# Where the weight chunks begin in SBUF: one offset for all jobs, or one for each layer and kind of job

## Chip, cores and metric

The kernel runs on one core of one Trainium2 chip. The metric is device microseconds of one execution, as the median of several runs.

## What is computed

A decoder trunk of two layers on one sequence of 256 tokens and 2048 channels, all in float32. Each layer normalises its input, projects it to 7692 columns, runs three mixers on parts of them (a convolution module, a gated delta rule, a dilated window attention), gates and concatenates their outputs and projects them back:

```
for l in range(DEPTH):
    h = rms_norm(x, norm_w[l])
    u = h @ w_in[l].astype(h.dtype)
    ...
    y = jnp.concatenate([y_conv, y_gdn, y_att], axis=-1)
    x = x + y @ w_out[l].astype(y.dtype)
return rms_norm(x, final_norm_w)
```

The convolution module has one more product, of 512 by 512 (`conf_pw_w`). The change touches the big products alone: `h @ w_in`, the 512 by 512 one, and `y @ w_out`.

## The kernel before

**Three products for one.** Every float32 operand of a big product is split into a high part (rounded to float32r) and a low part (what is left). A matmul of the reference becomes three float32r matmuls into the same PSUM tile: high by high, low by high, high by low. The activations stand in SBUF as `HT` (normalised input) and `YT` (mixer outputs), two tiles each, high and low, with the channels on the partitions: 16 blocks of 128 channels, each a slice of 256 tokens (1024 bytes).

**Weights.** They come from HBM in chunks of 128 partitions, two blocks of 128 rows each (one block each for the first two chunks of the program's first job), by SP's DMA queue into one of four `RAW` buffers. `split_weights` (lines 414 to 430) then has ACT write the high part into one of three `WHI` buffers (tile `whi`, line 191) and DVE the low part into one of three `WLO` buffers (tile `wlo`, line 199). A chunk fills its buffer from the buffer's first byte (line 422); the second block of a chunk follows the first at n x 4 bytes, n being the job's columns (384, 512, 396 or 256).

**Jobs.** `project` (line 468) walks through a list of jobs; each is one block of weight columns against all 16 (for `conf_pw_w` 4) blocks of channels. `unit` (line 442, its matmuls at line 455) is one block of 128 channels in one job. There are two kinds:

- channel-row jobs (`chan` is True): the result has channels on its rows. The weights are the stationary operand, 128 columns at a time, and 256 tokens of `HT` or `YT` move. The trace names them `acc<-HT,whi` and `acc<-HT,wlo` (moving operand first). They are the convolution's and the delta rule's inputs, the attention gate and `conf_pw_w`.
- token-row jobs (`chan` is False): the result has tokens on its rows. 128 tokens of `HT` or `YT` are stationary, and 384, 396, 512 or 256 weight columns move: `acc<-whi,HT` and the like. They are the gate `GZ` (384 and 396 columns), the attention's q, k and v, and `w_out`.

Each matmul has its own weight load (PEld), which runs while the matmul before it still streams its moving operand. The program's very last job (`"last"`) keeps its split weights in the two `HT` tiles, which are free by then; its matmuls are at line 464 and don't use `WHI` and `WLO`.

**Order.** A planner (`Plan`) writes the order of all engines from fixed costs: whichever task can start first goes next. Small matmuls and transposes of the mixers (lines 232, 239 and 754, tiles `mix`) are put between the units of the jobs.

**Addresses.** In bytes of a partition: `HT` and `YT` begin at 18432, 34816, 51200 and 67584, all multiples of 512; the four `raw` buffers at multiples of 4096 past 100352, also multiples of 512. `gap0` (64 bytes, line 263) lies before the weight buffers, so the six of them begin 64 bytes past a multiple of 512 (the first at 116800, then every 4096 bytes). `gap1` (448 bytes) brings the tiles behind them back to multiples of 512 (`b768_0` at 141824). 128 columns of float32 are 512 bytes, and so are the steps between stationary slices, tokens and channel blocks multiples of 512; in the 396-column job alone the chunk's second block begins 1584 bytes on, 48 more than a multiple of 512.

Of the kernel before, what the change touches and what calls it, by code (L numbers as in the profile page):

```python
# [11 lines left out]
F32 = mybir.dt.float32  # L12
F32R = mybir.dt.float32r
# [162 lines left out]
def hybrid_trunk(ctx, tc, x, x_t, w_in, conf_pw_w, w_out, params, final_norm_w, rope, lnc, out):  # L176
    nc = tc.nc
    cp = ctx.enter_context(tc.tile_pool(name="consts", bufs=1))
    wp = ctx.enter_context(tc.tile_pool(name="weights", bufs=1))
# [74 lines left out]
    def many(n, cols, name, dt=F32, pool=None):  # L254
        return Slots([(pool or sp).tile([128, cols], dt, name=f"{name}{i}", tag=f"{name}{i}") for i in range(n)])
# [4 lines left out]
    HT = [cp.tile([128, KB, S], F32R, name=f"HT{i}") for i in range(2)]  # L260
    YT = [cp.tile([128, KB, S], F32R, name=f"YT{i}") for i in range(2)]
    RAW = Slots([wp.tile([128, 1024], F32, name=f"raw{i}") for i in range(4)])
    wp.tile([128, 16], F32, name="gap0")
    WHI = Slots([wp.tile([128, 1024], F32R, name=f"whi{i}") for i in range(3)])
    WLO = Slots([wp.tile([128, 1024], F32R, name=f"wlo{i}") for i in range(3)])
    wp.tile([128, 112], F32, name="gap1")
    S768 = many(14, 768, "b768_")
    S1024 = many(3, 1024, "b1024_")
    S512 = many(2, 512, "b512_")
# [79 lines left out]
    chunks = []  # L349
    raw_ready, w_ready, w_gone = [], [], []  # L350

    def add_chunks(w, c0, n, order, keep):


        first = len(chunks)
        wt, rows, base = w
        base += rows * c0
        for k, m in order:
            src = bass.AP(tensor=wt.tensor, offset=wt.offset + base + (k // 2) * 256 * n + (k % 2) * n,
                          ap=[[2 * n, 128]] + ([[256 * n, m // 2]] if m > 2 else []) + [[1, min(m, 2) * n]])  # L360
            chunks.append((src, m, n, k if keep else None))
            for lst in (raw_ready, w_ready):
                lst.append([Event(), None])
        return first

    def load_xt(k0, m):

        buf = yield ("get", S768)
        yield ("dma", 128 * m * S * 4 / 330.0, lambda: nc.sync.dma_start(  # L369
            buf[:, :m * S], bass.AP(tensor=x_t.tensor, offset=x_t.offset + k0 * S, ap=[[KB * S, 128], [1, m * S]])))  # L370
        plan.spawn(norm_xt(k0, m, buf), 2)
# [9 lines left out]
    def load_x(j):  # L381

        c0, n = X_PIECES[j]
        buf = yield ("get", S768)
        xs = buf[:, :NT * n].rearrange("p (t c) -> p t c", t=NT)
        yield ("dma", 128 * NT * n * 4 / 330.0, lambda: nc.sync.dma_start(
            xs, xf[:, c0:c0 + n].rearrange("(t p) c -> p t c", p=128)))
        plan.spawn(sums_x(j, xs, buf), 3)
        if j == len(X_PIECES) - 1:
            nc.sync.dma_start(lncs, lnc)  # L390
            nc.sync.dma_start(ropes, rope.rearrange("(t p) c -> p t c", p=128))
# [4 lines left out]

    def load_weights(order):
        for i in order:
            src, m, n, _ = chunks[i]
            if i in XT_BEFORE:  # L400
                yield from load_xt(*XT_BEFORE[i])
            if i in X_BEFORE:
                yield from load_x(X_BEFORE[i])
            raw = yield ("get", RAW)
            view = raw[:, :m * n].rearrange("p (a n) -> p a n", n=n)
            flat_ = raw[:, :m * n]
            if m > 2:
                flat_ = flat_.rearrange("p (a n) -> p a n", n=2 * n)
            raw_ready[i][1] = (raw, view)
            yield ("dma", 128 * m * n * 4 / 330.0,  # L410
                   lambda src=src, flat_=flat_: nc.sync.dma_start(flat_, src))  # L411
            yield ("set", raw_ready[i][0])

    def split_weights(order):
        for i in order:
            src, m, n, keep = chunks[i]
            yield ("wait", raw_ready[i][0])
            raw, view = raw_ready[i][1]
            if keep is None:
                hb = yield ("get", WHI)  # L420
                lb = yield ("get", WLO)
                hi, lo = (b[:, :m * n].rearrange("p (a n) -> p a n", n=n) for b in (hb, lb))
                w_ready[i][1] = (hi, lo, hb, lb)
            else:
                hi, lo = (b[:, keep:keep + m, :] for b in HT)
                w_ready[i][1] = (hi, lo, None, None)
            e = Event()
            plan.spawn(split_hi(hi, view, e), 0)
            plan.spawn(split_lo(i, hi, lo, raw, view, e), 0)
            yield ("wait", e)  # L430

    def split_hi(hi, view, e):
        yield act(hi, view)
        yield ("set", e)

    def split_lo(i, hi, lo, raw, view, e):
        yield ("wait", e)
        yield tt(lo, view, hi.bitcast(F32), ALU.subtract)
        yield ("put", RAW, [raw])
        yield ("set", w_ready[i][0])  # L440

    def unit(acc, hi, lo, a, n, A, k, first, last, chan):


        def emit():
            for t in range(n // 128 if chan else NT):
                s = slice(t * 128, (t + 1) * 128)
                if chan:
                    o = acc[t // 2][:, (t % 2) * S:(t % 2 + 1) * S]
                    terms = [(hi[:, a, s], A[0][:, k, :]), (hi[:, a, s], A[1][:, k, :]), (lo[:, a, s], A[0][:, k, :])]  # L450
                else:
                    o = acc[t][:, :n]
                    terms = [(A[0][:, k, s], hi[:, a, :n]), (A[1][:, k, s], hi[:, a, :n]), (A[0][:, k, s], lo[:, a, :n])]
                for i, (w, m) in enumerate(terms):
                    nc.tensor.matmul(o, w, m, start=first and i == 0 and not (chan and t % 2), stop=last and i == 2,  # L455
                                     skip_group_check=chan)
        return ("pe", 6 * (n / 2.4 + 2.5), emit)

    def last_unit(acc, t, k, n):

        def emit():
            s = slice(t * 128, (t + 1) * 128)
            for i, (w, m) in enumerate(((0, 0), (1, 0), (0, 1))):
                nc.tensor.matmul(acc[t][:, :n], YT[w][:, k, s], HT[m][:, k, :n], start=k == 0 and i == 0,  # L464
                                 stop=k == KB - 1 and i == 2)
        return ("pe", 3 * (n / 2.4 + 2.5), emit)

    def project(jobs):


        todo = [(j, add_chunks(j[2], j[3], j[4], j[5], j[9] == "last")) for j in jobs]
        order = list(range(len(chunks)))
        if jobs[-1][9] == "last":
            tail = order[todo[-1][1]:]
            at_ = todo[-3][1]
            order = order[:at_]
            for i in range(at_, todo[-1][1]):
                order.append(i)
                if i % 2 and tail:
                    order.append(tail.pop(0))  # L480
            order += tail
        plan.spawn(load_weights(order), 0)
        plan.spawn(split_weights(order), 0)
        for (A, ready, w, c0, n, order, then, prio, before, chan), first in todo:
            if before:
                plan.spawn(before, 1)
            acc = yield ("get", ACC)
            if chan == "last":
                for t in range(NT):
                    for k in range(KB):  # L490
                        yield ("wait", w_ready[first + k // 4][0])
                        yield last_unit(acc, t, k, n)
                    plan.spawn(then(acc, t), prio)
                return
            for i, (k0, m) in enumerate(order):
                yield ("wait", w_ready[first + i][0])
                hi, lo, hb, lb = w_ready[first + i][1]
                for a in range(m):
                    k = k0 + a
                    yield ("wait", ready[k])  # L500
                    yield unit(acc, hi, lo, a, n, A, k, i + a == 0, i == len(order) - 1 and a == m - 1, chan)
                yield ("put", WHI, [hb])
                yield ("put", WLO, [lb])
            plan.spawn(then(acc), prio)
# [765 lines left out]
    for l in range(DEPTH):  # L1270
        jobs, bg = layer(l)
        all_jobs += jobs
        for gen, prio in bg:
            plan.spawn(gen, prio + 10 * l)
    plan.spawn(project(all_jobs), 50)
    plan.run()

# [60 lines left out]
```

## Time and profile before

| | |
|---|---|
| median of 3 runs | 972.93 us (972.45 to 974.32) |
| the profiled execution | 972.88 us, span 971.2 us |
| mean granted TensorE clock | 0.997 of 2.4 GHz |
| PE busy | 958.6 us, 99% |
| DVE, ACT, POOL busy | 748.1, 550.8, 48.6 us |
| DMA, mean over the span | 184 GB/s |

The span runs from the first to the last instruction in the profile; the execution's time has 1.7 us more around it. PE's busy time is a union of modelled matmul durations that overlap (a matmul is shown with some 160 ns more than the distance to the next), so the pace of the matmuls has to be read from their starts or their counts in a stretch of time, not from the busy time.

### The profile page before, as it was taken

What the parts mean: (1) busy time and instruction counts of PE and PEld (TensorE: products, weight loads), DVE (VectorE), ACT (ScalarE), POOL (GpSimd) and SP (SyncE); (2) the same over time, 40 slices, a digit from 0 to 9 for tenths busy, and PEclk for the clock granted to TensorE, in tenths of its full rate; (3) what the DMA queues carried; (4) which work ended last, traced back from release to release, by engine and by line L of the source; (5) the groups of instructions that cost most, each with busy time, mean ns of one, the idle gap of its engine ahead of it and who ended that gap; (6) DMA issues with size and microseconds to landing.
All of it is one profiled execution on the core that took longest, in us unless ns stands there. A gap on an engine that the chain in (4) does not pass through costs nothing.

```text
span 971.2 us, 19060 instructions
## 1 busy us (share of the span) xinstructions
PE 958.6 (99%) x7259; PEld 937.3 (97%) x7259; DVE 748.1 (77%) x1519; ACT 550.8 (57%) x1079; POOL 48.6 (5%) x70
## 2 busy tenths in 40 slices
PE   8999999999999999999999999999999999999996
PEld 8999999999999999999899999999899999999996
DVE  7697799999999666655558768999999976666672
ACT  7774355446685764554456634564466767544551
POOL 1002100200010000000000020002000100000000
PEclk9999999999999999999999999999999999999998
DMA  9865565644445535776666555556344556467772
GB/s 325 261 201 170 175 192 183 187 148 146 148 138 173 183 114 185 222 244 219 215 194 196 196 168 172 188 181 196 123 149 142 151 186 203 125 194 218 221 252 88
DMA packets 67037, 179.01 MB, mean 184 GB/s; under 512 B 8000, under 2 KB 12224, under 8 KB 66944
## 3 DMA queue, kind: packets, MB, share of 16 engines
q1 hardware_dynamic: 64880, 173.85, 55.6%
q0 software_dynamic: 1632, 3.02, 1.2%
q8 instruction: 57, 0.93, 0.4%
q10 hardware_dynamic: 432, 0.91, 0.3%
q14 instruction: 36, 0.29, 0.1%
HBM read 172.77 MB, written 4.98 MB: 183 GB/s over the span
## 4 chain that ended last, share of the span: by engine, by line
PE 97%; DVE 1%; DMA 1%; issue 1%; SPq 0%; ACT 0%; POOLq 0%; POOL 0%; DVEq 0%; ACTq 0%
PE acc L455 87%; PE mix L232 6%; PE mix L239 3%; DMA b<-in_x_t 1%; PE acc L464 1%; PE mix L754 0%; DVE wlo L199 0%; DVE b L196 0%; SPq L411 0%; SPq L369 0%; DVE inv L212 0%; ACT whi L191 0%; POOLq L1334 0%; POOL rstd L248 0%; DVE PTs L206 0%
## 5 line engine op out<-in xcount | busy, mean ns | idle before, releaser
L191 ACT ACTIVATE whi<-raw 128x768 fp32r<-128x768 f32 (+4 forms) x389 | 339.9, 874 | 352.5 <-PE acc L455 313.0
L199 DVE TENSOR_TENSOR wlo<-raw,whi 128x768 fp32r<-128x768 f32 (+4 forms) x389 | 385.2, 990 | 178.9 <-ACT whi L191 174.8
L455 PE MATMUL acc<-HT,whi 128*128 128x256 f32 x2304 | 404.7, 280 | 0.0
L455 PEld LDWEIGHTS acc<-HT,whi 128*128 128x128 f32 x2304 | 350.4, 189 | 1.5 <-issue 1.5
L455 PE MATMUL acc<-HT,wlo 128*128 128x256 f32 x1152 | 320.5, 278 | 0.0
L455 PE MATMUL acc<-whi,HT 128*128 128x384 f32 (+1 forms) x1024 | 270.8, 346 | 1.1 <-ACT whi L191 1.1
L455 PEld LDWEIGHTS acc<-HT,wlo 128*128 128x128 f32 x1152 | 216.3, 188 | 0.0
L455 PEld LDWEIGHTS acc<-whi,HT 128*128 128x128 f32 x1024 | 180.2, 189 | 3.4 <-ACT whi L191 1.5
L455 PE MATMUL acc<-wlo,HT 128*128 128x384 f32 (+1 forms) x512 | 173.1, 338 | 0.6 <-DVE wlo L199 0.6
L455 PE MATMUL acc<-whi,YT 128*128 128x384 f32 (+2 forms) x640 | 161.8, 336 | 0.0
L196 DVE SCALAR_TENSOR_TENSOR b<-b,par,b 128x255 f32<-128x255 f32 (+20 forms) x348 | 153.6, 465 | 0.3
L455 PEld LDWEIGHTS acc<-whi,YT 128*128 128x128 f32 x640 | 113.9, 188 | 2.4
L455 PE MATMUL acc<-wlo,YT 128*128 128x384 f32 (+2 forms) x320 | 107.5, 336 | 0.0
L455 PEld LDWEIGHTS acc<-wlo,HT 128*128 128x128 f32 x512 | 96.3, 188 | 1.6 <-DVE wlo L199 1.6
L455 PEld LDWEIGHTS acc<-wlo,YT 128*128 128x128 f32 x320 | 60.1, 188 | 1.4
L191 ACT ACTIVATE b<-mix 128x384 f32<-128x384 f32 (+3 forms) x96 | 39.6, 425 | 19.2 <-PE mix L232 12.3
L232 PE MATMUL mix<-b,b 128*128 128x128 f32 (+5 forms) x456 | 45.9, 285 | 0.0
L239 PE MATMUL mix<-ident,b 128*128 128x128 f32 x280 | 45.8, 274 | 0.0
L232 PEld LDWEIGHTS mix<-b,b 128*128 128x128 f32 (+3 forms) x456 | 36.2, 161 | 6.6 <-issue 2.2
L239 PEld LDWEIGHTS mix<-ident,b 128*128 128x128 f32 x280 | 34.1, 141 | 3.8 <-issue 1.3
L196 DVE SCALAR_TENSOR_TENSOR b<-b,b 128x256 f32<-128x256 f32 (+3 forms) x62 | 31.5, 510 | 2.5 <-ACT b L191 2.3
L191 ACT ACTIVATE b<-b,stat 128x128 f32<-128x128 f32 (+1 forms) x68 | 29.1, 442 | 6.0 <-DVE stat L206 5.9
(146 smaller groups left out, 612.9 us busy)
## 6 DMA issues: line engine op xcount, KB each, us to landing
raw<-in_w_in SPq DMA_DIRECT2D x240, 384.0 KB, 3.0
raw<-in_w_in SPq DMA_DIRECT2D x48, 512.0 KB, 3.9
raw<-in_w_out SPq DMA_DIRECT2D x64, 384.0 KB, 3.5
raw<-in_w_out SPq DMA_DIRECT2D x12, 512.0 KB, 4.1
raw<-in_w_in SPq DMA_DIRECT2D x15, 396.0 KB, 3.7
b<-in_x SPq DMA_DIRECT2D x10, 256.0 KB, 5.4
raw<-in_conf_pw_w SPq DMA_DIRECT2D x4, 512.0 KB, 3.2
raw<-in_w_out SPq DMA_DIRECT2D x8, 256.0 KB, 3.6
```

Source lines behind the costliest of these rows:

```text
L191: lambda: nc.scalar.activation(out_, in_, func, bias=bias, scale=scale, **kw))
L196: lambda: nc.vector.scalar_tensor_tensor(out_, a, s, b, op0=op0, op1=op1))
L199: return ("dve", 70 + _free(out_) / 0.96, lambda: nc.vector.tensor_tensor(out_, a, b, op=op))
L232: nc.tensor.matmul(o, a, b, start=f[0], stop=f[1])
L239: nc.tensor.transpose(o, a, ident)
L455: nc.tensor.matmul(o, w, m, start=first and i == 0 and not (chan and t % 2), stop=last and i == 2, skip_group_check=chan)
L464: nc.tensor.matmul(acc[t][:, :n], YT[w][:, k, s], HT[m][:, k, :n], start=k == 0 and i == 0, stop=k == KB - 1 and i == 2)
```

## The change

The three buffers of each weight pool become 128 columns (512 bytes) longer, `gap0` and `gap1` go, and a table `SKEW` gives the first column of a chunk in its buffer by layer (its key's first part: whether the weights' base offset is above zero, which is so in the second layer) and kind of job (its second: whether it is a channel-row job). The buffers now begin at 116736, 121344 and so on, all multiples of 512, so a chunk begins 8 x 4 = 32 bytes past one in channel-row jobs of the first layer, 480 in its token-row jobs, 96 and 416 in the second layer's. The tiles behind the weight buffers move up by 2560 bytes (`b768_0` to 144384); those before them stay. The last job's table entry is not used, since its weights go to `HT`. The order of the instructions on every engine, with their waits, is the same as before.

```diff
--- before.py
+++ after.py
@@ -260,10 +260,9 @@
     HT = [cp.tile([128, KB, S], F32R, name=f"HT{i}") for i in range(2)]
     YT = [cp.tile([128, KB, S], F32R, name=f"YT{i}") for i in range(2)]
     RAW = Slots([wp.tile([128, 1024], F32, name=f"raw{i}") for i in range(4)])
-    wp.tile([128, 16], F32, name="gap0")
-    WHI = Slots([wp.tile([128, 1024], F32R, name=f"whi{i}") for i in range(3)])
-    WLO = Slots([wp.tile([128, 1024], F32R, name=f"wlo{i}") for i in range(3)])
-    wp.tile([128, 112], F32, name="gap1")
+    SKEW = {(False, True): 8, (False, False): 120, (True, True): 24, (True, False): 104}
+    WHI = Slots([wp.tile([128, 1024 + 128], F32R, name=f"whi{i}") for i in range(3)])
+    WLO = Slots([wp.tile([128, 1024 + 128], F32R, name=f"wlo{i}") for i in range(3)])
     S768 = many(14, 768, "b768_")
     S1024 = many(3, 1024, "b1024_")
     S512 = many(2, 512, "b512_")
@@ -349,7 +348,7 @@
     chunks = []
     raw_ready, w_ready, w_gone = [], [], []
 
-    def add_chunks(w, c0, n, order, keep):
+    def add_chunks(w, c0, n, order, keep, skew):
 
 
         first = len(chunks)
@@ -358,7 +357,7 @@
         for k, m in order:
             src = bass.AP(tensor=wt.tensor, offset=wt.offset + base + (k // 2) * 256 * n + (k % 2) * n,
                           ap=[[2 * n, 128]] + ([[256 * n, m // 2]] if m > 2 else []) + [[1, min(m, 2) * n]])
-            chunks.append((src, m, n, k if keep else None))
+            chunks.append((src, m, n, k if keep else None, skew))
             for lst in (raw_ready, w_ready):
                 lst.append([Event(), None])
         return first
@@ -396,7 +395,7 @@
 
     def load_weights(order):
         for i in order:
-            src, m, n, _ = chunks[i]
+            src, m, n, _, _ = chunks[i]
             if i in XT_BEFORE:
                 yield from load_xt(*XT_BEFORE[i])
             if i in X_BEFORE:
@@ -413,13 +412,13 @@
 
     def split_weights(order):
         for i in order:
-            src, m, n, keep = chunks[i]
+            src, m, n, keep, skew = chunks[i]
             yield ("wait", raw_ready[i][0])
             raw, view = raw_ready[i][1]
             if keep is None:
                 hb = yield ("get", WHI)
                 lb = yield ("get", WLO)
-                hi, lo = (b[:, :m * n].rearrange("p (a n) -> p a n", n=n) for b in (hb, lb))
+                hi, lo = (b[:, skew:skew + m * n].rearrange("p (a n) -> p a n", n=n) for b in (hb, lb))
                 w_ready[i][1] = (hi, lo, hb, lb)
             else:
                 hi, lo = (b[:, keep:keep + m, :] for b in HT)
@@ -468,7 +467,7 @@
     def project(jobs):
 
 
-        todo = [(j, add_chunks(j[2], j[3], j[4], j[5], j[9] == "last")) for j in jobs]
+        todo = [(j, add_chunks(j[2], j[3], j[4], j[5], j[9] == "last", SKEW[j[2][2] > 0, j[9] is True])) for j in jobs]
         order = list(range(len(chunks)))
         if jobs[-1][9] == "last":
             tail = order[todo[-1][1]:]
```

## Rows read from the trace of the kernel before

**Rows 1.** The page: engines (busy us, share of the span, instructions) and the chain that ended last
```profile
span 971.2 us, 19060 instructions
...
PE 958.6 (99%) x7259; PEld 937.3 (97%) x7259; DVE 748.1 (77%) x1519; ACT 550.8 (57%) x1079; POOL 48.6 (5%) x70
...
PE 97%; DVE 1%; DMA 1%; issue 1%; SPq 0%; ACT 0%; POOLq 0%; POOL 0%; DVEq 0%; ACTq 0%
PE acc L455 87%; PE mix L232 6%; PE mix L239 3%; DMA b<-in_x_t 1%; PE acc L464 1%; PE mix L754 0%; DVE wlo L199 0%; DVE b L196 0%; SPq L411 0%; SPq L369 0%; DVE inv L212 0%; ACT whi L191 0%; POOLq L1334 0%; POOL rstd L248 0%; DVE PTs L206 0%
```

**Rows 2.** Waits of PE: who waited for whom, us in total, times, longest
```profile
PE mix L318 <- POOL pw_neg L323: 1.6, 1, 1.6
PE acc L455 <- ACT whi L191: 1.1, 1, 1.1
PE acc L455 <- DVE wlo L199: 0.6, 2, 0.4
```

**Rows 3.** Tile wlo on PE: names, count, duration ns min/median/max, first and last start, forms (sampled)
```profile
L455 PE MATMUL acc<-HT,wlo x1152: 276/276/288, 26.1 to 873.2; 128*128 128x256 f32 x192
L455 PE MATMUL acc<-wlo,HT x512: 331/336/533, 5.5 to 803.1; 128*128 128x384 f32 x150, 128*128 128x396 f32 x21
L455 PE MATMUL acc<-wlo,YT x320: 280/336/400, 393.7 to 951.1; 128*128 128x384 f32 x128, 128*128 128x512 f32 x16, 128*128 128x256 f32 x16
L455 PE MATMUL acc<-YT,wlo x32: 276/276/283, 352.5 to 838.3; 128*128 128x256 f32 x32
```

**Rows 4.** Windows of one kind of job: stretch, length us, PE busy us (count), clock, DMA share, GB/s
```profile
94.00:134.00 40.00, 40.00 (x355) 1.00 0.57 178
361.00:393.00 32.00, 32.00 (x274) 1.00 0.56 182
874.00:939.00 65.00, 65.00 (x377) 1.00 0.73 230
940.00:951.00 11.00, 11.00 (x96) 1.00 0.42 146
```

**Rows 5.** Tile wlo (duration ns min/median/max) and its group, 25.7 to 393.2, then 502.9 to 873.2 us
```profile
L455 PE MATMUL acc<-HT,wlo x576: 276/276/283, 26.1 to 393.2; 128*128 128x256 f32 x192
L455 PE MATMUL acc<-wlo,HT x225: 331/336/342, 25.6 to 323.1; 128*128 128x384 f32 x112, 128*128 128x396 f32 x1
...
L455 PE MATMUL acc<-HT,wlo 128*128 128x256 f32 x576 | 159.9, 278 | 0.0
...
L455 PE MATMUL acc<-HT,wlo x575: 276/281/288, 503.3 to 872.9; 128*128 128x256 f32 x192
...
L455 PE MATMUL acc<-HT,wlo 128*128 128x256 f32 x575 | 160.3, 279 | 0.0
```

**Rows 6.** Timeline of PE, the last job: start us, length us, line, names, shapes, count
```profile
951.21 11.66 PE L464 MATMUL acc<-HT,YT 128*128 128x256 f32 x96
```

**Rows 7.** Timeline of PE at 57.4 us (lowr pair) and at 323.1 us (change of job)
```profile
57.55 0.51 PE L754 MATMUL mix<-r,lowr 128*128 128x384 f32 x2
57.90 0.28 PE L455 MATMUL acc<-HT,whi 128*128 128x256 f32 x1
...
323.11 0.34 PE L455 MATMUL acc<-wlo,HT 128*128 128x384 f32 x1
323.29 0.40 PE L455 MATMUL acc<-HT,whi 128*128 128x256 f32 x2
```

**Rows 8.** Timeline of PE in the 396-column job of layer two
```profile
490.84 0.53 PE L455 MATMUL acc<-whi,HT 128*128 128x396 f32 x2
...
491.95 0.52 PE L455 MATMUL acc<-whi,HT 128*128 128x396 f32 x2
...
493.03 0.38 PE L239 MATMUL mix<-ident,rstd 128*128 128x128 f32 x2
```

## Prediction

> **What bounds the kernel now.** I began with the engine table and the chain that ended last [rows 1]: PE is busy 99% of the span of 971.2 us and holds 97% of the chain. What PE waited longest for in total is 1.6, 1.1 and 0.6 us, 1.7 of it for weight halves [rows 2]. So the time is PE's own pace, and a change is worth what it does to the spacing of matmuls, count by count. The groups of tile wlo, which one of every three matmuls uses, give the counts [rows 3]: 3 x (1152 + 32) = 3552 matmuls in channel-row jobs (stationary W, 256 columns of HT or YT moving), 1776 a layer, and 3 x (512 + 320) = 2496 in token-row jobs (stationary HT or YT, W moving), 1248 a layer in 13 jobs, of which 11 have 384 columns.
>
> The spacing is read from windows that hold one kind of job and little else. Such a window also counts the matmuls alive at its left edge (a duration divided by a spacing, two or so), which I take off. 40 us at 94 us hold 355 - 2.4 channel-row matmuls: 113.4 ns each. 32 us at 361 us hold 274 - 2.4 of the very same shape: 117.8 ns [rows 4]. So channel-row jobs have two paces, **free** (113.4) and **held** (117.8), the displayed durations being 276 and 281 ns. In layer one the median duration is 276 and the mean 278, in layer two 281 and 279 [rows 5]: with 5 ns between the two states, about 0.4 of layer one and 0.6 of layer two is held. Mean spacing now: 113.4 + 0.4 x 4.4 = 115.1 ns and 113.4 + 0.6 x 4.4 = 116.0 ns. Token-row jobs of 384 columns run at 65 us / (377 - 1.9) = 173.3 ns, those of 256 columns at 11 / (96 - 2.4) = 117.5 [rows 4]; their shortest durations are 331 ns where the median is 336 [rows 5], so a state about 5 ns quicker exists there too, but is rare.
>
> Nothing waits, so what differs is how the weight load of the next matmul and the moving columns of this one meet in SBUF. I call **distance** the start of the next stationary slice minus the start of the current moving slice, modulo 512 bytes. HT and YT lie on multiples of 512, W 64 bytes past one, so the distance is +64 in channel-row and -64 in token-row jobs. The last job has both operands in HT and YT, distance 0: 96 matmuls in 11.66 us, 119.8 ns [rows 6], 2.3 above its neighbour of the same size at -64. With 384 columns, the last matmul before a change from token-row to channel-row (moving and next stationary both 64 past) is spaced 0.18 us; the pair of lowr matmuls, first at distance 0, second at +64, takes 0.35 us for both, so about 0.178 and 0.172 [rows 7]. So 0 is the worst distance seen, and +64 and -64 cost the same with 384 columns.
>
> **The change, part by part.** It moves no instruction: engines, order, waits, DMAs and buffer counts stay. HT, YT and raw keep their addresses; every tile behind the weights moves up by 2560 bytes, five times 512, so its place modulo 512 stays, and I cost that at nothing (these tiles feed the L232, L239 and L754 matmuls, a tenth of the chain). ACT's writes of whi and DVE's of wlo now start off a multiple of 64. No row shows such writes; PE waited 1.7 us for them in the whole span [rows 2], so even some ns on each stays hidden, and if the cover were gone PE would show waits for whi and wlo. What is left is the distance: +32 in layer one and +96 in layer two, for both kinds of job.
>
> 1. Channel-row, layer one, +64 to +32: 1776 matmuls. Bounds: all free, 113.4 (1776 x -1.7 = -3.0 us); all as at distance 0, 119.8 (1776 x +4.7 = +8.3 us). +32 lies midway between a distance that allows the free pace and one where 96 matmuls in a row showed none of it. I take no free pace, and midway between 117.8 and 119.8: 118.8, so 1776 x 3.7 = **+6.6 us**.
> 2. Channel-row, layer two, +64 to +96: away from the bad distance. Bounds: all free, 1776 x -2.6 = -4.6 us; all at 119.8, 1776 x +3.8 = +6.7 us. No row has +96. The nearest row is today's mixture, so **0**.
> 3. Token-row, layer one, -64 to +32: 1248 matmuls. With 384 columns 0 costs 178 and +64 some 173; midway 175.5 against 173.3 is 1248 x 2.2 = **+2.7 us**. Lower bound the quick state, 1248 x -5 = -6.2 us. For the upper bound the 396-column job helps: its second row of W starts 112 past a multiple of 512, 48 past one of 64, and six matmuls from 490.84 to 491.95 take 185 ns each; the next six, 64 past, take 180 [rows 8]. Scaled from 384 columns, (173.3 - 117.5) / 128 x 12 = 5.2 ns more would be 178.5. So a moving slice off its 64-byte line can cost 6.5 ns: +8.1 us.
> 4. Token-row, layer two, -64 to +96: nearest rows -64 and +64, equal, so **0**, with bounds -6.2 and +8.1 us as before.
>
> Sum: 6.6 + 0 + 2.7 + 0 = +9.3 us on the profiled execution's 972.88 us (span 971.2 and 1.7 around it; the median of three runs is 972.93): **982.2 us**. All lower bounds together give 952.9, all upper ones 1004.1.
>
> **Rivals.**
> A. *The free pace spreads* (faster). If today's held stretches are a phase in which load and stream run into each other and that +64 only narrowly avoids, another distance may avoid it always. For it: the same jobs run at both paces, so the free one needs no other instructions, only another start; runs of hundreds of matmuls keep either pace [rows 4]. Against it: distance 0 shows none of it, and 384 columns cost the same at both signs. Place: the 3552 channel-row matmuls; price -3.0 - 4.6 = -7.6 us, 965.3; with the token-row jobs in their quick state too, -20 us, 952.9. It decides from the point where over half of layer one's channel rows stay free, for then term 1 is about zero and any gain in layer two shows. If only +96 does it, -4.6 - 6.2 against +9.3 leaves 971.4.
> B. *Lines of 64 bytes* (slower by more). Both new offsets are 32 past a multiple of 64. If it is this that slowed the 396-column row, all 2496 token-row matmuls pay 6.5 ns, +16.2 us, and with term 1 the time is 995.7. For it: [rows 8]. Against it: that row's distance, -112, is its own too, and the rows do not separate the two.
> C. *Nothing happens*: 972.9. If loads and streams do not meet in SBUF, where W starts is of no account, and the two paces have another cause.
>
> The Trainium skill states C's rule: "TensorE: Matmul & The Clock Gate", in "Step-by-step: what each phase is for", gives PE two independent SBUF read ports and says that loading the next weights takes no read bandwidth from the running matmul; by it the time stays 972.9. The trace does not agree fully, 119.8 against 117.5 ns for equal work at distances 0 and -64.
>
> **How the numbers follow.** Runs of this kernel spread by some 0.2% (2 us), which is what a measurement can tell from no change. The likeliest case is the sum above, 0.42, with a range of its own from 976 to 990. A has 0.33 in all its forms, since the free state is known to exist and only its condition is not; B 0.13; C 0.12. Faster by over 0.2%: 0.33 (A). Within: 0.12 (C). Slower: 0.42 + 0.13 = 0.55. The range is 957 to 994: it takes in A down to nearly all its gain and the forecast's own range, and leaves out A's last few us and B's upper half, about 0.15.
>
> **What would show it.** Windows of one kind of job in the new profile: channel rows in layer one near 118.8 ns with a median duration over 281, none at 276; layer two as now; token rows near 175 ns in layer one and 173 in layer two; the last job, whose operands do not move, still 11.66 us; PE's waits for whi and wlo unchanged. Wrong if layer one's channel rows keep stretches at 113.4, if token rows go under 170 or over 178, or if any wait on PE grows.

## Result and profile after

The changed kernel takes **983.35 us** (median of 4 runs, 983.02 to 985.38) against 972.99 of the kernel before (4 runs, 972.45 to 974.32): ratio 1.0109, interval 1.0093 to 1.0125. It is slower by 10.4 us; the forecast was 982.2 us. Of the 19 executions of the kernel before that ran beside e1 to e4 below, one took 1726.49 us and stands outside the ratios; their median is 972.82.

The page of the kernel after: engines (busy us, share of the span, instructions) and the chain that ended last, to be read against [rows 1].

```profile
span 983.7 us, 19060 instructions
...
PE 970.7 (99%) x7259; PEld 948.6 (96%) x7259; DVE 749.2 (76%) x1519; ACT 550.8 (56%) x1079; POOL 48.3 (5%) x70
...
PE 97%; DVE 1%; issue 1%; DMA 1%; SPq 0%; ACT 0%; POOLq 0%; POOL 0%; DVEq 0%; ACTq 0%
```

The instructions are the same in number, PE holds the same 97% of the chain, and its busy time has grown by 12.1 us, about the 12.5 us by which the span grew. The other engines are where they were. The waits of PE (who waited for whom, us in total, times, longest), against [rows 2]:

```profile
PE acc L454 <- ACT whi L191: 1.7, 2, 1.3
PE mix L317 <- POOL pw_neg L322: 1.6, 1, 1.6
PE mix L232 <- DVE PTs L206: 0.6, 1, 0.6
PE acc L454 <- DVE wlo L199: 0.4, 1, 0.4
```

Waits give 0.4 us of it (whi and wlo together 2.1 us, 1.7 before). So PE does the same work at a slower pace. Where, the starts of the first big matmul of each stage tell (timeline of PE, differences of successive starts, us; "channel 1" is the eight channel-row jobs on `HT`, "channel 2" the later ones, on `HT` and on `conf_pw_w`):

| stage | layer one before | after | layer two before | after |
|---|---|---|---|---|
| ahead of the first big matmul | 4.7 | 4.6 | | |
| token rows, 396 columns | 21.1 | 22.4 | 18.6 | 18.5 |
| channel 1 | 150.0 | 155.2 | 151.7 | 154.4 |
| token rows, the others ahead of w_out | 147.5 | 147.9 | 148.5 | 148.8 |
| channel 2 | 70.0 | 71.2 | 70.0 | 70.8 |
| token rows, w_out | 91.2 | 91.6 | 77.9 | 78.3 |

The last job and the end take 20.0 us in both. The differences sum to 12.5 us: channel rows +6.4 in layer one and +3.5 in layer two, token rows without the 396-column jobs +0.8 and +0.7, the 396-column jobs and the time ahead of the first +1.1. This profiled execution is the 985.38 us one; the other three lie between 983.02 and 983.41, so about 2 us of the 12.5 belong to it alone, the longer start among them: there PE was busy for 6.67 of the first 10 us (7.16 before), and in the next 10 us the granted clock was 0.83 (1.00 before), so for a part of them it was at 1.2 GHz.

Now the pace. The chain of the kernel after, cut at four stretches (start us, us, what), shows long rows of matmuls that nothing interrupts:

```profile
97.07 42.95 PE acc L454 x363
...
368.19 33.22 PE acc L454 x279
...
579.67 34.38 PE acc L454 x293
...
885.96 64.48 PE acc L454 x372
```

The first is channel rows at +32: 42.95 / 363 = 118.3 ns. The second is the same (33.22 / 279 = 119.1, with the last few matmuls ahead of the change of job in it). The third is channel rows at +96: 117.3 ns, which about two thirds of layer two's channel rows have; the other stretches there run at 118.7, and all together at 117.8 on average. The fourth is token rows with 384 columns at +96: 173.3 ns. Before, the first stretch was at the free pace and the third at the held one:

```profile
93.72 41.50 PE acc L455 x366
...
569.62 44.52 PE acc L455 x378
...
873.86 67.15 PE acc L455 x390
```

41.50 / 366 = 113.4 ns and 44.52 / 378 = 117.8 ns in channel rows; the last of these lines is token rows, 384 columns but for its last few: 172.2 ns, the 173.3 of [rows 4] with those few in it. Tile wlo on PE, layer one (26.9 to 401.2 us) and layer two (511.3 to 885.3 us) of the kernel after (count, duration ns min/median/max):

```profile
L454 PE MATMUL acc<-HT,wlo x576: 274/281/288, 27.2 to 401.1; 128*128 128x256 f32 x192
L454 PE MATMUL acc<-wlo,HT x225: 333/336/345, 26.8 to 329.9; 128*128 128x384 f32 x112, 128*128 128x396 f32 x1
...
L454 PE MATMUL acc<-HT,wlo x575: 277/280/287, 511.6 to 885.0; 128*128 128x256 f32 x192
```

Against [rows 5] the channel rows' median went from 276 to 281 in layer one; in layer two it went from 281 to 280, but nothing stands at 276 any more (minimum 277). Taken matmul by matmul from the starts, some 68% of layer one's channel rows and 44% of layer two's lay in stretches of the free pace before; after, none in either layer. The loss of that pace is most of the result.

### The profile page after: what moved, and what is told of

Read it like the earlier page. It is cut to its first block, busy times and chain, and to the rows that moved or that the text cites. A ratio compares the mean times of both kernels' runs of the same rounds, so it can differ in the third digit from the quotient of the medians.

```text
span 983.7 us, 19060 instructions
## 1 busy us (share of the span) xinstructions
PE 970.7 (99%) x7259; PEld 948.6 (96%) x7259; DVE 749.2 (76%) x1519; ACT 550.8 (56%) x1079; POOL 48.3 (5%) x70
## 4 chain that ended last, share of the span: by engine, by line
PE 97%; DVE 1%; issue 1%; DMA 1%; SPq 0%; ACT 0%; POOLq 0%; POOL 0%; DVEq 0%; ACTq 0%
PE acc L454 87%; PE mix L232 6%; PE mix L239 3%; PE acc L463 1%; DMA raw<-in_w_in 1%; PE mix L753 0%; DVE wlo L199 0%; DVE b L196 0%; SPq L368 0%; DVE inv L212 0%; ACT whi L191 0%; SPq L410 0%; POOLq L1333 0%; POOL rstd L248 0%; DVE PTs L206 0%
## 5 line engine op out<-in xcount | busy, mean ns | idle before, releaser
L454 PE MATMUL acc<-HT,whi 128*128 128x256 f32 x2304 | 414.1, 282 | 0.0
L239 PE MATMUL mix<-ident,b 128*128 128x128 f32 x280 | 45.8, 274 | 0.0
L239 PEld LDWEIGHTS mix<-ident,b 128*128 128x128 f32 x280 | 34.1, 140 | 3.7 <-issue 1.4
```

The costliest lines, as they stand in the source:

```text
L239: nc.tensor.transpose(o, a, ident)
```

## Experiments

**The theory (distance):** what counts is the start of the stationary slice against the start of the moving slice, modulo some power of two; +64 alone allows the free pace. **Rival (lines):** an operand that starts off a multiple of 64 bytes is slow by itself (B of the prediction). **Second rival (window):** the cost falls smoothly around the best distance, so a neighbour of +64 does as well or better (A in another form).

### Which kind of job pays: e1 and e2

Channel-row jobs get their old +64 back, token rows stay changed:

```diff
-    SKEW = {(False, True): 8, (False, False): 120, (True, True): 24, (True, False): 104}
+    SKEW = {(False, True): 16, (False, False): 120, (True, True): 16, (True, False): 104}
```

> Channel-row chunks back at 64 bytes past a multiple of 512 in both layers, token-row chunks as changed (480 and 416). Theory: the loss is the channel rows' (6.4 us in layer one, 3.5 in layer two by the two profiles), so the stretches at 113.4 ns return and the time is 973 to 974.5 us; the 512-column job keeps its 233 ns instead of 229 (+0.4 us). Rival: the token rows carry about 3 us as I predicted for them, then 975.5 us or more.

Measured: 971.87 us (10 runs, 971.65 to 972.83) against 972.82 of the kernel before beside it, ratio 0.9990, interval 0.9981 to 1.0000. The whole loss is gone, and the tiles behind the weight buffers, which stay 2560 bytes further up in e1, carry none of it. The time is 1.1 us under the range that was expected. By the starts of the stages (as in the table above), the token rows do cost 0.8 us in layer one and 0.3 in layer two, but layer two's channel rows take 1.5 us less than in the kernel before, since more of them are free (64% against 44%), and the first 396-column job 0.9 us less. The other half, token rows at their old -64 and channel rows changed:

```diff
-    SKEW = {(False, True): 8, (False, False): 120, (True, True): 24, (True, False): 104}
+    SKEW = {(False, True): 8, (False, False): 16, (True, True): 24, (True, False): 16}
```

> Token-row chunks back at 64 bytes past a multiple of 512, channel-row chunks as changed (32 and 96). Theory: 982 to 983 us, channel rows at 117.3 ns in layer two and near 118 in layer one. Rival that the token rows carry a share: 980 us or less.

Measured: 983.77 us (4 runs, 983.10 to 983.81), ratio 1.0104, interval 1.0088 to 1.0120. By the stages the channel rows cost 6.3 us in layer one and 4.5 in layer two, and the token rows are where they were. So the channel rows carry nearly all of the loss, and the token rows about 1 us. Chain of e1, then of e2 (start us, us, what):

```profile
93.06 41.50 PE acc L454 x366
...
360.16 33.94 PE acc L454 x284
...
569.94 42.86 PE acc L454 x378
```

```profile
95.81 43.31 PE acc L454 x366
...
577.62 45.36 PE acc L454 x378
```

e1 has the free pace (113.4 ns) at 93 us and also at 570 us, where the kernel before was held (117.8); e2 is at 118.3 in layer one and at 120.0 in layer two. So +96 has paces of its own, 117.3 and 118.7 in the kernel after and here, 120.0 in this one long row, and none of them is free.

### Distance or line: e3

Everything that the big matmuls read moves by 32 bytes together: `HT` and `YT` begin 32, the weights 96 past multiples of 512, all distances as in the kernel before. Made from the kernel before:

```diff
-    cp.tile([128, PAD[0]], F32, name="pad0")
+    cp.tile([128, PAD[0] + 8], F32, name="pad0")
...
+    cp.tile([128, 120], F32, name="pad2")
...
-    wp.tile([128, 16], F32, name="gap0")
+    wp.tile([128, 24], F32, name="gap0")
...
-    wp.tile([128, 112], F32, name="gap1")
+    wp.tile([128, 104], F32, name="gap1")
```

> The kernel before with HT, YT and all weight buffers moved up by 32 bytes, so that every operand of a big matmul starts 32 bytes past a 64-byte line while all distances between stationary and moving stay +64 and -64. Distance theory: 973 us as before, stretches at 113.4 ns in both layers. Line theory (starts off a 64-byte line cost the free pace): no stretch under 117 ns, 981 to 985 us.

Measured: 973.03 us (10 runs, 972.36 to 973.63) against 972.82, ratio 0.9999, interval 0.9989 to 1.0008. The line rival falls: every operand of every big matmul starts off a multiple of 64, and nothing is lost. What has moved is which stretch is free (windows of PE: stretch, length, busy, count, clock, DMA share, GB/s):

```profile
94.00:134.00 40.00, 40.00 (x342) 1.00 0.59 171
363.00:393.00 30.00, 30.00 (x267) 1.00 0.64 184
```

With the 2.4 matmuls of the left edge taken off, the first gives 117.8 ns, held, where [rows 4] has 113.4, and the second 113.4, free, where [rows 4] has 117.8. The same instructions at the same distances thus run at either pace; a stretch keeps the one in which it begins until the mixers' small matmuls interrupt it. What chooses at the start was not found. It does not look like chance: of layer one's 16 stretches of 30 matmuls or more, 15 have the same pace in e1 as in the kernel before.

### Other distances: e4 to e11

Each takes another table `SKEW` with a pair of channel-row distances, one for each layer, and a pair for the token rows. Each ran once.

```diff
e4   SKEW = {(False, True): 32, (False, False): 32, (True, True): 48, (True, False): 48}
e5   SKEW = {(False, True): 12, (False, False): 112, (True, True): 20, (True, False): 116}
e6   SKEW = {(False, True): 14, (False, False): 124, (True, True): 18, (True, False): 126}
e7   SKEW = {(False, True): 15, (False, False): 4, (True, True): 17, (True, False): 8}
e8   SKEW = {(False, True): 10, (False, False): 0, (True, True): 22, (True, False): 12}
e9   SKEW = {(False, True): 80, (False, False): 64, (True, True): 112, (True, False): 96}
e10  SKEW = {(False, True): 6, (False, False): 24, (True, True): 26, (True, False): 104}
e11  SKEW = {(False, True): 26, (False, False): 16, (True, True): 40, (True, False): 16}
```

> All chunks begin 128 bytes past a multiple of 512 in layer one and 192 in layer two, multiples of 64, so channel-row distances are +128 and +192, token-row ones -128 and -192. Distance theory: the free pace belongs to a window near +64, so channel rows run at 117 to 118 ns in both layers, 980 to 984 us, token rows at 173.3 ns. Line theory: the free pace comes back in both layers, 973 us or less.

> Channel-row distances +48 in layer one and +80 in layer two; token-row distances +64 and +48. Theory (a window of distances near +64 in which the stream stays clear of the weight load): if the window reaches 16 bytes to each side, stretches at 113.4 ns stay in both layers, 970 to 975 us; if it is narrower, 117 to 118 ns, 980 to 984 us. Rival (each distance has its own pace, with no window): layer one and two differ without order. Token rows: 173.3 ns at both, as at -64, +32 and +96.

> Channel-row distances +56 and +72; token-row distances +16 and +8. Window theory: both have stretches at 113.4 ns, and on the side towards the middle of the window the held ones are rarer; 968 to 976 us if token rows stay at 173.3 ns. Token rows: near distance 0 they should rise towards the 177 ns seen in single matmuls, by at most 4 ns or 4.6 us a layer.

> Channel-row distances +60 and +68, one column to each side of the kernel before; token-row distances -16 and -32. Window theory: held and free stretches as before in both layers, within 2 us of them. If the exact multiple of 64 matters, there are none at 113.4 ns. Token rows: 173.3 to 177 ns, rising towards distance 0.

> Channel-row distances +40 and +88, near the edges +32 and +96 at which no stretch was free; token-row distances 0 and -48. Window theory: 117 to 120 ns in both layers, 981 to 985 us for the channel rows' part; a free stretch in one of the two tells on which side the window is wider. Token rows at 0: 177 ns if the single matmuls at distance 0 tell of many, +4.6 us in layer one; at -48 173 to 175 ns.

> Channel-row distances +320 (64 + 256) in layer one and 448, which is -64, in layer two; token-row distances -256 and +128. So far the free pace was seen at +64 and +88 alone, and not at 32, 40, 48, 56, 60, 68, 72, 80, 96, 128 or 192. If the banks repeat every 256 bytes, layer one has stretches at 113.4 ns; if every 512, none, and 117 to 120 ns. If the sign does not matter, layer two has both paces, 113.4 and 117.8; if the weight load has to start ahead of the stream, none at 113.4. Token rows: 173.3 to 176 ns.

> Channel-row distances +24 and +104, both 8 past a multiple of 16 as +88 was; token-row distances -96 and +96. Theory that the free pace goes with single distances in phase with the load (64, then 88, then more at steps of 8 or 16 above it): one of the two, rather +104, has stretches at 113.4 ns. Theory of no order near 64: neither, 117 to 120 ns. Token rows: 173.3 ns at +96 as in the changed kernel, and at -96 if multiples of 32 are alike.

> Channel-row distances +104 in layer one and +160 (which is -96 modulo 256) in layer two; token rows at -64 as in the kernel before. The runs so far show the free pace at +64, +88 and +320, hardly at 192 and not at the other distances. Theory that free distances are single ones on the near side of +96: neither has it, 117 to 120 ns, 978 to 984 us. Theory that there are more of them at steps of 8 above 88: layer one has stretches at 113.4 ns, and then its channel rows take 206 to 208 us as in the kernel before.

Measured, with the kernel before beside it (the paces are the spacings of starts within uninterrupted stretches; two values where both occur; "free" is the share of the layer's channel rows at the free pace):

| kernel | us, before | distance layer one: ns, free | distance layer two: ns, free |
|---|---|---|---|
| before | 972.99 | +64: 113.3 or 117.8, 68% | +64: the same, 44% |
| after | 983.35, 972.99 | +32: 118.3, none | +96: 117.3 or 118.7, none |
| e1 | 971.87, 972.82 | +64: 113.3 or 117.8, 68% | +64: the same, 64% |
| e2 | 983.77, 972.82 | +32: 118.3, none | +96: 117.3, 118.7 or 120.0, none |
| e3 | 973.03, 972.82 | +64: 113.3 or 117.8, 54% | +64: the same, 57% |
| e4 | 987.45, 972.82 | +128: 118.7, none | +192: 117.8, 2% |
| e5 | 988.63, 972.41 | +48: 117.8 or 118.3 (one row 123.3), none | +80: 118.7, none |
| e6 | 990.88, 972.41 | +56: 117.8 on average, uneven, none | +72: 118.3 on average, none |
| e7 | 989.44, 972.41 | +60: 119.5 on average, none | +68: 118.3, none |
| e8 | 981.73, 972.41 | +40: 119.2, none | +88: 116.7 or 113.3, 39% |
| e9 | 979.01, 973.06 | +320: 113.3 or 117.8, 61% | +448: 117.8, 5% |
| e11 | 987.01, 975.00 | +104: 117.8 or 120.0, none | +160: 120.0, none |

The times of e4, e5 and e11 lie 3 to 5 us above the ranges expected for no free pace. In e4 and e5 the token rows alone cost 4.8 and 4.9 us by the stages, and in e11 layer two's channel rows, at +160, have 120.0 ns throughout.

The window rival falls: four bytes to either side of +64 (e7) no stretch is free. Chain of e7 at +60, then at +68 (119.5 and 118.3 ns):

```profile
96.06 43.73 PE acc L454 x366
...
581.87 43.19 PE acc L454 x365
```

The free pace was seen in long stretches at +64, at +88 and at +320, which is 64 + 256. The 512 bytes in my definition are therefore more than is needed: 256 fits the pairs that were run. These are +64 and +320; +192 and +448 (117.8 ns, hardly ever free, both); for token rows 0 and -256 (below), and -128 and +128 (176 ns on average, both). A repeat of 128 does not fit: +64 and +192 are 128 apart and run differently. Chain of e8 in layer two, then of e9 in both layers:

```profile
577.67 44.10 PE acc L454 x378
...
628.37 10.24 PE acc L454 x90
```

```profile
93.55 41.50 PE acc L454 x366
...
571.53 44.52 PE acc L454 x378
```

e8 at +88 begins at 116.7 ns and, after an interruption, goes on at 113.8, the free pace with its edges. e9 at +320 has 113.4 in layer one, the very stretch of the kernel before; its second line is +448 in layer two, 117.8. At +88 fewer stretches are free than at +64, but the others have 116.7 where +64 has 117.8: layer two's channel rows take 221.1 us by the stages in e8 against 221.7 in the kernel before, so +88 costs no more than +64.

The token-row distances ran along: with 384 columns the long rows have 173.3 ns at -64, +32, +96, 0 and -256, 175.6 at -16 and 179.9 at +16. Only at -64 have the short stretches 173.3 too; at the others of these some run at 174 to 177, and at +64, +48, +8, -32, -48, -128, +128 and -192 the stretches lie at 173.3 to 177 ns, seldom at 178. Chain of e8 (token rows at 0) and of e6 (at +16), 96 matmuls of w_out in layer one between two groups of mixer work:

```profile
421.07 16.64 PE acc L454 x96
```

```profile
421.25 17.27 PE acc L454 x96
```

16.64 / 96 = 173.3 ns and 17.27 / 96 = 179.9. With 512 columns, which is one job, in layer one, -64 has 228.9, +32 233.4 and 0 and -256 have 226.7. e4 to e7 lose more than the kernel after partly by this: e6's token-row stages ahead of w_out and in w_out take 150.4 and 94.4 us in layer one, against 147.5 and 91.2 before.

e10 gives no verdict. Its one execution took 5423.56 us; PE waited no longer than elsewhere, but each big matmul was drawn out, as the timeline of PE (start us, length us, line) shows:

```profile
5180.33 2.26 PE L454 MATMUL acc<-whi,YT 128*128 128x384 f32 x2
5182.25 1.38 PE L454 MATMUL acc<-wlo,YT 128*128 128x384 f32 x1
5183.30 1.39 PE L454 MATMUL acc<-whi,YT 128*128 128x384 f32 x1
```

From 5180.33 to 5183.30 us three matmuls of 384 columns take 2.97 us, 990 ns each. These are token rows of layer two, whose table entry is that of the kernel after, and there they have 173.3 ns. The mixers' matmuls of L239 were drawn out as well (1039 ns as shown, 274 in the kernel before), though their operands did not move modulo 512 bytes, while DVE's writes of wlo took what they take elsewhere (993 ns against 990). So this was the execution and not the offset; its cause was not looked into. +104 was run again in e11 (117.8 or 120.0); +24 was not, and stays open.

No version beat the kernel before by more than can be told: e1, at 0.9990 with an interval up to 1.0000, is the nearest.

## Why the prediction was right

The direction, the cause and the size (forecast +9.3, measured +10.4 us) hold; two of the four terms were mis-sized, in opposite directions (by +3.5 and -1.9 us), so that the sum came this near is in part luck. The prediction says as a fact that load and stream meet in SBUF; the runs show that the two starts count relative to one another, not where or why.

1. **Channel rows, layer one: right.** Forecast 118.8 ns and +6.6 us; 118.3 ns and +6.4 us were measured, and "no free pace" is what the windows show. Both ends were half a ns too high (118.8 for 118.3, 115.1 for 114.6), which cancels. That the pace lay midway towards the 119.8 of distance 0 is not borne out as a rule: +40 has 119.2, +48 has 117.8 or 118.3, and +128 has 118.7.
2. **Channel rows, layer two: mis-sized.** The step was "The nearest row is today's mixture, so 0". There was no mixture of free and held at +96: the stretches run at 117.3 or 118.7 ns, 117.8 on average, against 113.3 x 0.44 + 117.8 x 0.56 = 115.8 before; 1776 x 2.0 = 3.6 us, and +3.5 us by the stage table. The free pace came at single distances only, so a new distance had to be counted as losing it. Of the sixteen other distances that the runs had in channel rows, twelve had no free stretch, +192 and +448 a few per cent, and only +88 and +320 much of it. In e2 the longest row at the same distance ran at 120.0 ns.
3. **Token rows, layer one: mis-sized.** The step was "With 384 columns 0 costs 178", read from single matmuls, one at a change of job and a lowr pair [rows 7]. In a long row, 0 has 173.3 ns (e8), as do -64, +32 and +96; the 0.178 us told nothing of these. +0.8 us by the stages in place of +2.7, of which the 512-column job's 4.5 ns a matmul (233.4 against 228.9) are 96 x 4.5 = 0.4 us; the rest fits the short stretches at 174 to 175.6 ns.
4. **Token rows, layer two: about right.** Forecast 0, measured +0.7 us in the one profiled execution, and +0.3 in e1 at the same distance.

The price of unaligned writes, costed at nothing, stayed hidden. The waits for whi and wlo grew by 0.4 us, which the prediction had named as a sign of being wrong, but e1 and e2, each with one kind of job's writes off a multiple of 64, have 1.0 and 1.1 us of such waits against the 1.7 before, and e3, with all of them off a multiple of 64, has 1.5. The last job, whose operands did not move, takes as long as in [rows 6] (start us, us, what, in the timeline of the kernel after):

```profile
963.69 11.67 PE L463 MATMUL acc<-HT,YT 128*128 128x256 f32 x96
```

**Rivals.** A (the free pace spreads) needed over half of layer one's channel rows free; none are. Another distance can allow it, as +88 does in 39% of a layer, but none allowed it more than +64 does, whose share lies between 44 and 68% of a layer in the kernel before, e1 and e3. B (lines of 64 bytes) fell in e3, and with it my reading of [rows 8]: in e3 every row of W is off its line, and the 396-column jobs take 20.9 and 18.6 us, no more than the 21.1 and 18.6 before. C (nothing happens) fell with the result and with e1 and e2 against each other. The rule of the Trainium skill on which C rested, "TensorE: Matmul & The Clock Gate", "Step-by-step: what each phase is for", that the two operands have independent read ports, does not carry as far as "where they start is of no account": e1 and e2 issue the same instructions, and the row of 366 near 94 us takes 41.50 us in one and 43.31 in the other. That the two reads meet in SBUF is my reading of it; what the runs show is only that the pace goes by the difference of the two starts and not by either one. Whether it is the next matmul's stationary slice or the running one's that counts, they do not tell, since within a job all slices of an operand start alike modulo 256 bytes (in all but the 396-column jobs).

**Open:** what puts a stretch at +64 into the free or the held pace when it begins (the kernel before, e1 and e3 differ in this at equal distances), why +88 shares the free pace while +80, +72 and +68 do not, and what +24 does.

## What to carry over

Where PE is the bound and each matmul has its own weight load, the starts of the two operands relative to one another were worth some 4% of a matmul here (113.3 to 118.3 ns with 256 columns) and belong in the address plan; take the pace from counts over long uninterrupted stretches, never from single matmuls. Two paces of one and the same instruction in a trace mean a state that a small change can lose: count what share runs at the better one before costing the change, and take that share as lost unless a run shows otherwise. A table of offsets by layer tries two values in one run.

## Unexpected in the hardware

- The pace is not a smooth function of the distance: +64 has 113.3 ns in long stretches, +60 and +68 never, +88 has it in part, and +320 repeats +64.
- Both paces at +64 are stable: 366 matmuls in a row at 113.4 ns in the kernel before and in e1, the same 366 at 117.8 in e3, without a change within the row.
- Moving every operand by 32 bytes costs nothing (973.03 against 972.82 us), and moving one against the other by 32 costs 1.1%.
- The order of the distances depends on the number of columns: with 256 token-row columns -32 is quicker than -64 (116.7 against 117.8 ns, e7 and the kernel before), with 384 it is not (173.3 to 177 against 173.3).
